# Splitting a pair of weight chunks in fewer, longer operations, from three long ring buffers

## The chip, the core and the metric

The kernel runs on one core of a Trainium2 chip. The time is the device time of one execution in microseconds; the profile is of one execution on the same core.

## The reference

A two-layer decoder trunk in float32, 256 tokens, width 2048, 16 heads of 128, hidden width 8192. Layer 0 mixes by a short gated convolution, layer 1 by stick-breaking attention over keys and values that are made from layer 0's output; each is followed by a squared-ReLU MLP, and every sub-layer stands between two RMS norms.

```python
def reference(x, a_w_in, a_conv_w, a_w_out, kv_norm_g, w_kv, b_w_q, b_w_o, ...):
    h = x
    for i in range(2):
        u = rmsnorm(h, mix_pre_g[i])
        if i == 0: # proj = u @ w_in; y = gate_b * conv3(gate_c * xin); y @ w_out
            m = short_conv_mixer(u, a_w_in[0], a_conv_w[0], a_w_out[0])
        else:      # q = u @ w_q; stick-breaking weights of q, k; (a @ v) @ w_o
            m = stick_breaking_mixer(u, b_w_q[0], k_sh, v_sh, b_w_o[0])
        h = h + rmsnorm(m, mix_post_g[i])
        u = rmsnorm(h, mlp_pre_g[i])
        h = h + rmsnorm(jnp.square(jax.nn.relu(u @ w_up[i])) @ w_down[i], mlp_post_g[i])
        if i == 0:
            k_sh, v_sh = split(rmsnorm(h, kv_norm_g) @ w_kv)
    return h
```

## The kernel before

All products with weights are made in a float32 of two parts. A number is split into a high part (rounded to the format that TensorE multiplies at full rate) and a low part (the number less its high part); a product is high x high, high x low and low x high, three matmuls into one PSUM bank. The activations are split once. The weights, some 400 MB, pass through the chip once and are split on the way.

**The stream.** All weights lie in HBM as chunks of 128 x 1024 float32 (512 KB) in the order of their use. `load_one` issues the load of the next chunk on the SP queue into one of 5 raw tiles (`RAW`). `high_parts` makes a chunk's high part on ScalarE (L173) and `low_part` the low part on VectorE (L184, or L186 where a gain is multiplied in), into one of 7 tiles each (`RING`). `chunk(i)`, called where TensorE's matmuls are written, first writes down the splits up to chunk i + 4 (`AHEAD`; i + 2 in the first chunks). A split waits for its ring slot, which comes free when the last matmul on it is done. A raw tile comes free when its readers are done, and its next load follows.

**Pairs in seven products.** Where two consecutive chunks are a pair, they hold the four 128 x 512 quarters b11, b12 (first chunk), b21, b22 (second) of a block that is multiplied with four blocks of activations by the Strassen-Winograd scheme: 7 products in place of 8, 21 matmuls. The activations' sums are made by `four_sums`, the weights' differences by `split_seven`: t1 = b12 - b11, t3 = b22 - b12, t2 = b22 - t1, t4 = b21 - t2, each a 128 x 512 operation on VectorE (L210) into a tile `sums` that exists once. Then come four splits in four ring slots: a (b11 alone, half a slot), b (the whole second chunk, b21 and b22), t (t1, t2), u (t3, t4): four ScalarE operations (L218), four VectorE operations (L184). `seven_products` lists the products in the order b11, b21, b22, t1, t2, t3, t4.

**Where pairs stand.** In the convolution's projection 16 pairs alternate with 16 of the 26 tiles of output features (a tile takes two chunks; matmuls L748, pairs L857 to L859); a tile's bank is emptied by a ScalarE copy of one half (L755) and a VectorE addition (L757), and the same bank 6 serves every tile between pairs. In each MLP the down-projection's pairs (L1120 to L1122) alternate with tiles of the up-projection (32 matmuls, L1013 high and L1020 low); a tile's bank is emptied by L1026 (ScalarE) and L966 (VectorE) and bank 2 serves every tile. An MLP has 51 pairs in seven products, a few in eight. Partial results of a pair's products are added in SBUF by DMAs from the POOL queue (L1030).

**Order of the work.** TensorE's order is as written. The other engines are ordered by a scheduler at build time, by priority (order of writing, with some blocks raised), and each then runs its queue in order. At the transitions between sub-layers VectorE and ScalarE run in written order too: `Norms.begin` splits up to a limit, `allow(n)` raises it, and `at(delay, ...)` places steps by a planned clock that `spent` advances; with `apart` set, low parts are written separately by `low_parts`.

Of the kernel before, what the change touches and what calls it, by code (L numbers as in the profile page):

```python
# [12 lines left out]
ALU = mybir.AluOpType  # L13
# [82 lines left out]
def trunk(ctx, tc, x, xT, vecs, rows, ws, out):  # L96
# [45 lines left out]

    raw, parts, early = {}, {}, {}
    last_load = [None]
    count = {"loaded": 0, "split": 0, "limit": 1 << 30, "apart": False}
    lows = []
    sevens = {}

    def load_one():
        i = count["loaded"]  # L150
        if i >= len(stream):
            return
        w, c = stream[i]
        t = wpool.tile([P, CW], F32, tag="raw", name=f"raw{i}")
        n = HALF if i < FIRST else CW
        for a in range(0, CW, n):
            last_load[0] = nc.sync.dma_start(t[:, a : a + n], w.ap[c, :, a : a + n])
        raw[i] = t
        count["loaded"] += 1

    def pieces_of(i):
        w, c = stream[i]
        gains = w.gains(c) if w.gains else [None] * (4 if i < FIRST else 1)
        n = CW // len(gains)
        return [(slice(j * n, (j + 1) * n), gain) for j, gain in enumerate(gains)]

    def high_parts(i):
        while count["loaded"] <= i:
            load_one()
        hi = wsplit.tile([P, CW], F32R, tag="hi", name=f"whi{i}")  # L170
        lo = wsplit.tile([P, CW], F32R, tag="lo", name=f"wlo{i}")
        for j, (at, gain) in enumerate(pieces_of(i)):
            rounded = nc.scalar.activation(  # L173
                hi[:, at], raw[i][:, at], AF.Copy, scale=1.0 if gain is None else gain
            )
            if j < 2:
                early[i] = rounded
            if not count["apart"]:
                low_part(hi, lo, raw[i], at, gain)
        parts[i] = hi, lo  # L180

    def low_part(hi, lo, t, at, gain):
        if gain is None:
            nc.vector.tensor_tensor(lo[:, at], t[:, at], hi[:, at].bitcast(F32), op=ALU.subtract)  # L184
        else:
            nc.vector.scalar_tensor_tensor(  # L186
                lo[:, at], t[:, at], gain, hi[:, at].bitcast(F32), op0=ALU.mult, op1=ALU.subtract
            )

    def low_parts(until=None):  # L190

        while lows and (until is None or lows[0] <= until):
            i = lows.pop(0)
            for at, gain in pieces_of(i):
                low_part(*parts[i], raw[i], at, gain)
            raw.pop(i)
            load_one()
            if until is None:
                break

    def split_seven(i):

        while count["loaded"] <= i + 1:
            load_one()
        a, b = raw.pop(i), raw.pop(i + 1)
        sums = sevens[i].tile([P, 4, HALF], F32, tag="gpre", name="sums", bufs=1)
        t1, t2, t3, t4 = (sums[:, j, :] for j in range(4))
        b11, b12, b21, b22 = a[:, :HALF], a[:, HALF:], b[:, :HALF], b[:, HALF:]
        for t, x, y in ((t1, b12, b11), (t3, b22, b12), (t2, b22, t1), (t4, b21, t2)):
            nc.vector.tensor_tensor(t, x, y, op=ALU.subtract)  # L210
        factors = []
        for name, src in (("a", b11), ("b", b[:]), ("t", sums[:, 0:2, :]), ("u", sums[:, 2:4, :])):
            n = 1 if name == "a" else 2
            src = src if n == 1 or name == "b" else src.rearrange("p a b -> p (a b)")
            hi = wsplit.tile([P, CW], F32R, tag="hi", name=f"whi{i}{name}")
            lo = wsplit.tile([P, CW], F32R, tag="lo", name=f"wlo{i}{name}")
            at = slice(0, n * HALF)
            nc.scalar.activation(hi[:, at], src, AF.Copy)  # L218
            low_part(hi, lo, src, at, None)
            factors += [(hi[:, j * HALF : (j + 1) * HALF], lo[:, j * HALF : (j + 1) * HALF]) for j in range(n)]  # L220
        parts[i] = factors
        count["split"] += 2
        load_one()
        load_one()

    def split_one():
        i = count["split"]
        if i in sevens:
            split_seven(i)
            return  # L230
        high_parts(i)
        count["split"] += 1
        if count["apart"]:
            lows.append(i)
        else:
            raw.pop(i)
# [29 lines left out]
    def four_sums(to, a11, a21, a12, a22):  # L266
        s1, s2, s3, s4 = to
        for t, v, w, op in (
            (s1, a21, a22, ALU.add), (s2, s1, a11, ALU.subtract), (s3, a11, a21, ALU.subtract), (s4, a12, s2, ALU.subtract),
        ):  # L270
            nc.vector.tensor_tensor(t, v, w, op=op)

    def seven_products(x, sums, factors):

        b11, b21, b22, t1, t2, t3, t4 = factors
# [26 lines left out]
    def allow(n):  # L302

        count["limit"] += n
        while count["split"] <= count["limit"]:
            split_one()

    class Group:
# [29 lines left out]
        def both(self, i):  # L338

            for b in range(NB):  # L340
                self.unit(b, i)

        def last_units(self, b, edge):

            for c in range(2):
                for i in range(self.n - edge, self.n):
                    self.half(b, c, i)
                    if i == self.n - 1:
                        self.evict(b, c, self.ps.pop((b, c)))
                    spent(UNIT / 2)  # L350

    def run(groups, enter=False, leave=None):
# [3 lines left out]
        for b in range(NB):  # L356
            for gr, i in units[:first]:
                gr.unit(b, i)
        for gr, i in units[first:last]:
            if i == 0 and gr.start is not None:  # L360
                gr.start()
            gr.both(i)
# [343 lines left out]
    def convolution(tmp):  # L706
# [106 lines left out]
        for k in range(KD):  # L813
# [8 lines left out]
            elif k % 2 and k + 2 < KD:  # L822
                enter(k + 1)
                enter(k + 2)
            mm([(ps, k, n) for ps, n in zip(pss, IN_N[:LEAD])], lambda k, n: at_lead[k, n])
            if k % 2 and LATER <= k + 2 < KD:
                squares((k + 2 - LATER) // 2, k + 2)
# [23 lines left out]
        def pair(i):  # L851
# [4 lines left out]
            for key, (xh, xl), (hi, lo) in seven_products(x, sums[q], chunk(IN_AT["pair", i])):  # L856
                nc.tensor.matmul(group[key][:], xh, hi, start=q == 0, stop=False)  # L857
                nc.tensor.matmul(group[key][:], xh, lo, start=False, stop=False)
# [28 lines left out]
        for kind, i in IN_UNITS:  # L887
# [8 lines left out]
            behind = i < 4 or i >= KD + 4  # L896
            mm([(ps, k, n) for k in range(KD)], lambda k, n: at * CH + k, (1, 0) if behind and i % 2 == 0 else (0, 1))
            if not scale:
                statistics()
# [39 lines left out]
    def mlp(pool, i, before, after):  # L939
# [93 lines left out]
        def lead_up(to):  # L1033
# [7 lines left out]
            for k, n in alone:  # L1041
                low(first, place[k, n], k, n)
            for k in range(ALONE, KD):
                for n in lead:
                    high(first, place[k, n], k, n, n + 2)
                for n in lead:
                    low(first, place[k, n], k, n)
                    if k == KD - 1:
                        finish(to, n)
# [3 lines left out]
        def whole_up(to, n, first, number):  # L1053
            for k in range(KD):
                high(first, k, k, n, number)
            for k in range(KD):
                low(first, k, k, n)
            finish(to, n)

# [40 lines left out]
        class Down:  # L1100
# [40 lines left out]
            def seven(self, at, first, xs, n):  # L1141
                x = [[xs.x(n + j, b) for b in range(NB)] for j in range(2)]
                for key, a, w in seven_products(x, xs.sums[n], chunk(first)):
                    own = {1: "more", 5: "fifth", 6: "more", 7: "more"}.get(key, "sum")
                    self.products(key, own, at, [(a, w)])
                spent(3.5 * UNIT)

            def eight(self, at, first, xs, n):
# [12 lines left out]
                else:  # L1161
                    products((0, 1), "sum", lambda t: [xs.sums[n][:, t, j, :] for j in range(2)], 1)
                    products(5, "fifth", lambda t: xs.x(n + t, 1), 1)
                spent(4 * UNIT)

# [246 lines left out]


def banded(w, cols=CW):

# [61 lines left out]
```

## Time and profile before

| | us |
|---|---|
| median of three runs | 2111.22 |
| lowest, highest | 2110.32, 2113.54 |
| the profiled execution | 2110.45 |
| its span, first to last instruction | 2108.7 |

The profiled execution's own time includes about 1.75 us outside the span. The profile gives for each engine its busy time and number of instructions, for each group of instructions the source line, the tiles, the count, the summed and the mean time, and the idle time of the engine ahead of them with what ended it. Matmuls overlap their neighbours, and so do VectorE's and ScalarE's instructions at their ends: the time that one takes of its engine is read from start to start.

### The profile page before, as it was taken

To read this page: it belongs to the slowest core of one execution; us is meant where nothing else is said; L and a number is where in the kernel's file an instruction comes from. 1 tells how busy PE (TensorE), PEld (TensorE's weight loads), DVE (VectorE), ACT (ScalarE), POOL (GpSimd) and SP (SyncE) were. 2 spreads that over 40 slices of the span, in tenths; PEclk is the share of its full clock that TensorE was granted. 3 is DMA by queue.
4 is the path that set the end of the run, shared out by engine and by line. 5 is a ranking of instruction groups with operands and counts; after the bars stand their busy time and mean duration, and the time that the engine had idled before them with its cause. 6 is when DMAs were issued, how large, how long until landed. Compare 5 with 4: busy or idle time off the path is not lost.

```text
span 2108.7 us, 29835 instructions
## 1 busy us (share of the span) xinstructions
PE 2090.4 (99%) x10608; PEld 1782.2 (85%) x10608; DVE 1835.2 (87%) x2807; ACT 1435.2 (68%) x2210; POOL 113.7 (5%) x137
## 2 busy tenths in 40 slices
PE   9999999999999999999999999999999999999998
PEld 8888888888888888888888888889888888888886
DVE  9999965999899999999866777558989999999997
ACT  8656544776776776767567888547767767677674
POOL 0000000010110110101000000000101001011010
PEclk9999999999999999999999999999999999999999
DMA  8467574586777867868575555655778688687683
GB/s 290 155 205 250 191 259 142 190 244 213 232 230 223 265 194 236 250 205 268 173 222 165 160 160 166 218 175 170 199 237 238 213 239 242 210 255 215 220 267 137
DMA packets 132342, 449.23 MB, mean 213 GB/s; under 512 B 14816, under 2 KB 15072, under 8 KB 131168
## 3 DMA queue, kind: packets, MB, share of 16 engines
q1 hardware_dynamic: 113184, 406.55, 58.7%
q0 software_dynamic: 18720, 40.38, 9.9%
q8 instruction: 83, 1.36, 0.3%
q14 instruction: 67, 0.55, 0.1%
q10 hardware_dynamic: 288, 0.39, 0.1%
HBM read 413.19 MB, written 2.10 MB: 197 GB/s over the span
## 4 chain that ended last, share of the span: by engine, by line
PE 91%; DVE 6%; DMA 2%; issue 1%; ACT 1%; DVEq 0%; ACTq 0%
PE up L1013 20%; PE up L1020 11%; PE acc L326 8%; PE acc L328 8%; PE acc L327 8%; PE acc L748 5%; PE more L1121 4%; PE more L1120 4%; PE more L1122 4%; PE acc L1120 4%; PE acc L1121 4%; PE acc L1122 4%; PE lead L748 2%; DVE wlo L184 1%; DMA raw<-w_mlp 1%; PE up L1015 1%
## 5 line engine op out<-in xcount | busy, mean ns | idle before, releaser
L184 DVE TENSOR_TENSOR wlo<-raw,whi 128x1024 fp32r<-128x1024 f32 (+1 forms) x442 | 528.1, 1206 | 87.0 <-ACT whi L173 86.6
L173 ACT ACTIVATE whi<-raw 128x1024 fp32r<-128x1024 f32 (+1 forms) x442 | 453.0, 1043 | 171.1 <-PE acc L328 82.5
L1013 PE MATMUL up<-u,whi 128*128 128x512 f32 x1952 | 465.6, 390 | 3.5 <-DVE s L966 3.5
L1013 PEld LDWEIGHTS up<-u,whi 128*128 128x128 f32 x1952 | 364.6, 188 | 79.9 <-DVE s L966 5.4
L1020 PEld LDWEIGHTS up<-u,wlo 128*128 128x128 f32 x2048 | 263.6, 191 | 10.3
L1020 PE MATMUL up<-u,wlo 128*128 128x256 f32 x2048 | 268.0, 283 | 0.0
L1030 POOL DMA_DIRECT2D mg<-more x108 | 101.7, 1051 | 1280.5 <-ACT s L968 648.3
L186 DVE SCALAR_TENSOR_TENSOR wlo<-raw,gv,whi 128x512 fp32r<-128x512 f32 (+1 forms) x160 | 131.9, 854 | 41.5 <-ACT whi L173 40.8
L210 DVE TENSOR_TENSOR sums<-raw,sums 128x512 f32<-128x512 f32 x236 | 162.1, 687 | 1.3
L173 ACT ACTIVATE whi<-raw,gv 128x512 fp32r<-128x512 f32 (+1 forms) x160 | 121.6, 800 | 48.5 <-PE acc L328 41.8
L326 PE MATMUL acc<-whi,u 128*128 128x512 f32 x384 | 153.1, 399 | 0.1
L328 PE MATMUL acc<-whi,u 128*128 128x512 f32 x384 | 150.0, 391 | 0.0
L327 PE MATMUL acc<-wlo,u 128*128 128x512 f32 x384 | 149.8, 390 | 0.0
L1026 ACT ACTIVATE half<-up 128x256 f32<-128x256 f32 x128 | 48.5, 381 | 89.1 <-PE up L1020 85.5
L748 PE MATMUL acc<-u,whi 128*128 128x512 f32 x416 | 98.9, 391 | 2.7 <-DVE sum L757 2.7
L210 DVE TENSOR_TENSOR sums<-raw,raw 128x512 f32<-128x512 f32 x118 | 81.0, 687 | 23.2 <-DMA raw<-w_mlp 23.0
L967 ACT ACTIVATE s<-s 128x256 f32<-128x256 f32 x128 | 52.4, 413 | 66.3 <-DVE s L966 65.9
L748 PEld LDWEIGHTS acc<-u,whi 128*128 128x128 f32 x416 | 77.4, 188 | 20.5 <-DVE sum L757 3.7
L210 DVE TENSOR_TENSOR sums<-raw 128x512 f32<-128x512 f32 x118 | 81.0, 686 | 11.9 <-DMA raw<-w_mlp 11.7
L328 PEld LDWEIGHTS acc<-whi,u 128*128 128x128 f32 x384 | 72.1, 188 | 15.6
L326 PEld LDWEIGHTS acc<-whi,u 128*128 128x128 f32 x384 | 72.2, 188 | 13.8 <-ACT tk L1309 0.6
L327 PEld LDWEIGHTS acc<-wlo,u 128*128 128x128 f32 x384 | 72.3, 188 | 13.4
(5995 smaller groups left out, 4513.4 us busy)
## 6 DMA issues: line engine op xcount, KB each, us to landing
raw<-w_mlp SPq DMA_DIRECT2D x512, 512.0 KB, 4.6
raw<-w_in SPq DMA_DIRECT2D x94, 512.0 KB, 4.4
mg<-more POOLq DMA_DIRECT2D x108, 256.0 KB, 8.3
raw<-w_out SPq DMA_DIRECT2D x32, 512.0 KB, 4.5
raw<-w_v SPq DMA_DIRECT2D x32, 512.0 KB, 4.3
raw<-w_k SPq DMA_DIRECT2D x32, 512.0 KB, 4.4
raw<-w_q SPq DMA_DIRECT2D x32, 512.0 KB, 4.2
raw<-w_wo SPq DMA_DIRECT2D x32, 512.0 KB, 3.7
```

What stands on the lines that cost most here:

```text
L173: rounded = nc.scalar.activation(hi[:, at], raw[i][:, at], AF.Copy, scale=1.0 if gain is None else gain)
L184: nc.vector.tensor_tensor(lo[:, at], t[:, at], hi[:, at].bitcast(F32), op=ALU.subtract)
L210: nc.vector.tensor_tensor(t, x, y, op=ALU.subtract)
L326: nc.tensor.matmul(ps[:], xh, hi[:, a], start=i == 0 and k == 0, stop=False)
L327: nc.tensor.matmul(ps[:], xh, lo[:, a], start=False, stop=False)
L328: nc.tensor.matmul(ps[:], xl, hi[:, a], start=False, stop=i == self.n - 1 and k == self.ks - 1)
L748: nc.tensor.matmul(ps[:, :cols], w, xs[:, :cols], start=k == 0 and part == parts[0], stop=k == KD - 1 and part == parts[1], skip_group_che ...
L1013: nc.tensor.matmul(ps, weight(0, first, m), x, start=k == 0, stop=False)
L1020: nc.tensor.matmul(pss[n][:, :T], weight(1, first, m), x, start=False, stop=k == KD - 1)
L1120: nc.tensor.matmul(self.ps[key][:], xh, hi, start=first, stop=False)
L1121: nc.tensor.matmul(self.ps[key][:], xh, lo, start=False, stop=False)
L1122: nc.tensor.matmul(self.ps[key][:], xl, hi, start=False, stop=last)
```

## The change

The 5 raw tiles become one tile `raws` of 5 x 1024 columns, the 7 high and 7 low tiles one tile `his` and one tile `los` of 14 halves (512 columns) each. A chunk's raw place is its number modulo 5. Ring places are given out by halves in order of use (`ring_halves`), and a count of free halves is kept: `used(n)`, written after the matmuls that use them last, gives n halves back and calls `fill`, which writes down the next splits as long as the target is not reached and enough halves are free (2 for a chunk, 3 and then 4 for a pair). `chunk` and `allow` only raise the target and call `fill`.

A pair is split in two steps. `sums_of_weights` makes the differences, t1 and t3 in one operation of two rows where the pair's raw halves lie in a row, with b12 read by broadcast (t3 has the other sign, and so has its sum of activations in `four_sums`); then it splits b11, b21, b22 together, which is possible as the host now stores a pair's first chunk with its halves exchanged (b12, b11), so that the three lie in a row. When four halves are free, the second step splits the four differences: two high parts of 1024 columns, one low part of 2048. `runs` cuts an operation where the raw places or the ring places don't continue. The products' order is b11, b21, b22, t1, t3, t2, t4.

```diff
-    wpool = ctx.enter_context(tc.tile_pool(name="w", bufs=RAW))
-    wsplit = ctx.enter_context(tc.tile_pool(name="ws", bufs=RING))
+    wpool = ctx.enter_context(tc.tile_pool(name="w", bufs=1))
+    wsplit = ctx.enter_context(tc.tile_pool(name="ws", bufs=1))
...
+    raws = wpool.tile([P, RAW * CW], F32, name="raws")
+    his = wsplit.tile([P, 2 * RING * HALF], F32R, name="whi")
+    los = wsplit.tile([P, 2 * RING * HALF], F32R, name="wlo")
+
+    def raw_halves(i):
+        return [(raws, i % RAW * 2 + j) for j in range(2)]
+
+    def ring_halves(n):
+        assert count["free"] >= n
+        first = count["half"]
+        count["half"] += n
+        count["free"] -= n
+        return [(first + j) % (2 * RING) for j in range(n)]
...
+    def runs(src, dst):
+
+        k = 0
+        while k < len(src):
+            n = 1
+            while k + n < len(src) and all(
+                (src[k + n][0] is src[k][0], src[k + n][1] == src[k][1] + n, dst[k + n] == dst[k] + n)
+            ):
+                n += 1
+            yield src[k][0][:, src[k][1] * HALF : (src[k][1] + n) * HALF], slice(dst[k] * HALF, (dst[k] + n) * HALF)
+            k += n
...
-    def split_seven(i):
+    def sums_of_weights(i):
 
         while count["loaded"] <= i + 1:
             load_one()
-        a, b = raw.pop(i), raw.pop(i + 1)
-        sums = sevens[i].tile([P, 4, HALF], F32, tag="gpre", name="sums", bufs=1)
-        t1, t2, t3, t4 = (sums[:, j, :] for j in range(4))
-        b11, b12, b21, b22 = a[:, :HALF], a[:, HALF:], b[:, :HALF], b[:, HALF:]
-        for t, x, y in ((t1, b12, b11), (t3, b22, b12), (t2, b22, t1), (t4, b21, t2)):
-            nc.vector.tensor_tensor(t, x, y, op=ALU.subtract)
-        factors = []
-        for name, src in (("a", b11), ("b", b[:]), ("t", sums[:, 0:2, :]), ("u", sums[:, 2:4, :])):
...
-            nc.scalar.activation(hi[:, at], src, AF.Copy)
-            low_part(hi, lo, src, at, None)
...
+        (_, b12), (_, b11), (_, b21), (_, b22) = raw_halves(i) + raw_halves(i + 1)
+        sums = sevens[i].tile([P, 4 * HALF], F32, tag="gpre", name="sums", bufs=1)
...
+        if b22 == b11 + 2:
+            nc.vector.tensor_tensor(
+                total(0, 2).rearrange("p (a n) -> p a n", a=2),
+                of(b12).unsqueeze(1).to_broadcast([P, 2, HALF]),
+                of(b11, 3).rearrange("p (a n) -> p a n", n=HALF)[:, 0:3:2, :], op=ALU.subtract,
+            )
+        else:
+            nc.vector.tensor_tensor(total(0), of(b12), of(b11), op=ALU.subtract)
+            nc.vector.tensor_tensor(total(1), of(b12), of(b22), op=ALU.subtract)
+        nc.vector.tensor_tensor(total(2), of(b22), total(0), op=ALU.subtract)
+        nc.vector.tensor_tensor(total(3), of(b21), total(2), op=ALU.subtract)
+        begun.append(sums)
+        parts[i] = split_halves(raws, (b11, b21, b22), 1)
         load_one()
         load_one()
 
+    def split_halves(src, at, n_high):
+
+        halves = ring_halves(len(at))
+        src = [(src, j) for j in at]
+        n = len(at) // n_high
+        for a in range(0, len(at), n):
+            for x, to in runs(src[a : a + n], halves[a : a + n]):
+                nc.scalar.activation(his[:, to], x, AF.Copy)
+        for x, to in runs(src, halves):
+            low_part(x, to, None)
+        return [[ring[:, j * HALF : (j + 1) * HALF] for ring in (his, los)] for j in halves]
+
+    def needed():
+        return (4 if begun else 3) if count["split"] in sevens else 2
+
     def split_one():
         i = count["split"]
+        if begun:
+            parts[i] += split_halves(begun.pop(), range(4), 2)
+            count["split"] += 2
+            return
...
+    def fill():
+        while count["split"] <= min(count["target"], len(stream) - 1) and count["free"] >= needed():
+            split_one()
+
+    def used(halves=2):
+
+        count["free"] += halves
+        fill()
+
     def chunk(i, low=True):
-        while count["split"] <= min(i + (AHEAD if i >= CALM else 2), len(stream) - 1, max(i, count["limit"])):
-            split_one()
+        count["target"] = max(count["target"], min(i + (AHEAD if i >= CALM else 2), max(i, count["limit"])))
+        fill()
...
-            (s1, a21, a22, ALU.add), (s2, s1, a11, ALU.subtract), (s3, a11, a21, ALU.subtract), (s4, a12, s2, ALU.subtract),
+            (s1, a21, a22, ALU.add), (s2, s1, a11, ALU.subtract), (s3, a21, a11, ALU.subtract), (s4, a12, s2, ALU.subtract),
...
-            (1, x[0][0], b11), ((0, 0), x[1][0], b21), ((0, 1), s4, b22), (5, s1, t1), (6, s2, t2), (7, s3, t3),
+            (1, x[0][0], b11), ((0, 0), x[1][0], b21), ((0, 1), s4, b22), (5, s1, t1), (7, s3, t3), (6, s2, t2),
...
                 for key, a, w in seven_products(x, xs.sums[n], chunk(first)):
                     own = {1: "more", 5: "fifth", 6: "more", 7: "more"}.get(key, "sum")
                     self.products(key, own, at, [(a, w)])
+                    used(1)
...
+def second_first(pair):
+    return np.stack([np.concatenate([pair[0][:, HALF:], pair[0][:, :HALF]], axis=1), pair[1]])
```

The other matmul loops call `used` in the same way after a chunk's last matmul: the lead and the tiles of the convolution, `Group.both` and `last_units`, `lead_up`, `whole_up`, and pairs in eight products (4 halves at once).

More of the change, by code (lines that the diff above doesn't have):

```diff
@@ L169, in high_parts @@
             load_one()
[L170 to L175, printed above, removed]
+        halves = ring_halves(2)
+        parts[i] = Part(his, halves), Part(los, halves)
+        for j, (x, to, gain) in enumerate(pieces_of(i)):
+            rounded = nc.scalar.activation(his[:, to], x, AF.Copy, scale=1.0 if gain is None else gain)
             if j < 2:
@@ L193, in low_parts @@
             i = lows.pop(0)
-            for at, gain in pieces_of(i):
-                low_part(*parts[i], raw[i], at, gain)
-            raw.pop(i)
+            for x, to, gain in pieces_of(i):
+                low_part(x, to, gain)
             load_one()
@@ L304, in allow @@
         count["limit"] += n
-        while count["split"] <= count["limit"]:
-            split_one()
+        count["target"] = max(count["target"], count["limit"])
+        fill()
     class Group:
@@ L825, in convolution @@
             mm([(ps, k, n) for ps, n in zip(pss, IN_N[:LEAD])], lambda k, n: at_lead[k, n])
+            for _ in range(k * LEAD // CH, (k + 1) * LEAD // CH):
+                used()
             if k % 2 and LATER <= k + 2 < KD:
@@ L1445 @@
     arrays["w_in"] = np.concatenate([tiled(w_in, IN_LEAD)] + [
-        bands[2 * i : 2 * i + 2] if kind == "pair" else tiled(w_in, [(k, IN_TILES[i]) for k in range(KD)])
+        second_first(bands[2 * i : 2 * i + 2]) if kind == "pair" else tiled(w_in, [(k, IN_TILES[i]) for k in range(KD)])
         for kind, i in IN_UNITS
@@ L1460 @@
         downs = [banded(w) for w in np.split(a["mlp_w_down"][i], STEPS, axis=0)]
+        for e, down in enumerate(downs):
+            for h in range(2):
+                for m in SEVEN[e][h]:
+                    pair = slice(8 * band_of(e, h) + 2 * m, 8 * band_of(e, h) + 2 * m + 2)
+                    down[pair] = second_first(down[pair])
         arrays[f"w_mlp{i}0"] = ups[0]
```

71 lines of the change are left out of this document (48 added, 23 removed).

## Prediction

> **What bounds the kernel now.** I read the page first: the span, the engines' busy time, the slices, the chain.
>
> ```profile
> span 2108.7 us, 29835 instructions
> PE 2090.4 (99%) x10608; PEld 1782.2 (85%) x10608; DVE 1835.2 (87%) x2807; ACT 1435.2 (68%) x2210; POOL 113.7 (5%) x137
> DVE  9999965999899999999866777558989999999997
> PE 91%; DVE 6%; DMA 2%; issue 1%; ACT 1%; DVEq 0%; ACTq 0%
> ```
>
> TensorE is busy 99% of the span and the chain of waits is 91% TensorE. The change leaves every matmul in place, so the most that it can win is the time in which TensorE stands still. VectorE is busy 87% on average, but its slices are full in the convolution's second half and in both MLPs. So the second view was the sums by stage, the third TensorE's waits (matmul rows, then weight-load rows), and beside them the wait of the differences for loads.
>
> ```profile
> core 0: us, PE busy (x) PEld busy (x) DVE busy (x) ACT busy (x) POOL busy (x), PEclk, DMA share, GB/s
> 50.00:200.00 150.00, 147.28 (x757) 124.97 (x756) 149.92 (x234) 91.60 (x122) 1.23 (x2) 1.00 0.61 200
> 560.00:990.00 430.00, 430.00 (x2204) 368.82 (x2203) 407.62 (x591) 305.16 (x462) 40.12 (x46) 1.00 0.77 233
> ...
> PE acc L748 <- DVE sum L757: 4.7, 5, 1.9
> PE up L1013 <- DVE s L966: 3.5, 4, 1.8
> ...
> PEld acc L748 <- DVE sum L757: 5.8, 5, 2.2
> PEld up L1013 <- DVE s L966: 5.4, 5, 2.2
> ...
> DVE sums L210 <- DMA raw<-w_mlp: 34.7, 27, 2.7
> ```
>
> From 50 to 200 us VectorE has no idle time (149.92 of 150.00) and TensorE loses 150.00 - 147.28 = 2.7 us; in the middle of the first MLP TensorE loses nothing (430.00 of 430.00) and VectorE has 5% free (407.62). All that TensorE loses to VectorE is 4.7 + 3.5 = 8.2 us by the matmul rows, 5.8 + 5.4 = 11.2 us by the weight-load rows. Each is the same kind: a PSUM bank cannot be reused because VectorE adds its two halves (L757, L966) late. None of these rows is a wait for a weight part. The gain therefore ends at 8 to 11 us, however much VectorE work goes.
>
> **What the change removes.** The split of one pair of weight chunks in seven products is 4 differences and 4 low parts on VectorE, 4 high parts on ScalarE.
>
> ```profile
> L184 DVE TENSOR_TENSOR wlo<-raw,whi 128x1024 fp32r<-128x1024 f32 x434 | 525.0, 1221 | 86.7 <-ACT whi L173 86.4 <-issue 0.2
> L173 ACT ACTIVATE whi<-raw 128x1024 fp32r<-128x1024 f32 x434 | 450.1, 1054 | 170.8 <-PE acc L328 82.5 <-PE up L1013 30.4 <-DMA raw<-w_mlp 15.8
> L210 DVE TENSOR_TENSOR sums<-raw,sums 128x512 f32<-128x512 f32 x236 | 162.1, 687 | 1.3
> L210 DVE TENSOR_TENSOR sums<-raw,raw 128x512 f32<-128x512 f32 x118 | 81.0, 687 | 23.2 <-DMA raw<-w_mlp 23.0
> L210 DVE TENSOR_TENSOR sums<-raw 128x512 f32<-128x512 f32 x118 | 81.0, 686 | 11.9 <-DMA raw<-w_mlp 11.7
> ```
>
> So there are 118 pairs; by the loops 16 of them are in the convolution and 51 in each MLP. Merging two 512-column operations into one of 1024 takes 2 x 687 - 1221 = 153 ns off the busy sum. But neighbouring operations overlap in the profile, so the true saving is read from their starts:
>
> ```profile
> 705.97 0.69 DVE L210 TENSOR_TENSOR sums<-raw,raw 128x512 f32<-128x512 f32 x1
> 706.57 0.69 DVE L210 TENSOR_TENSOR sums<-raw,sums 128x512 f32<-128x512 f32 x1
> 707.17 0.69 DVE L184 TENSOR_TENSOR wlo262a<-raw,whi262a 128x512 fp32r<-128x512 f32 x1
> ...
> 708.59 1.22 DVE L184 TENSOR_TENSOR wlo262b<-raw,whi262b 128x1024 fp32r<-128x1024 f32 x1
> 709.72 1.22 DVE L184 TENSOR_TENSOR wlo262t<-sums,whi262t 128x1024 fp32r<-128x1024 f32 x1
> 710.85 1.22 DVE L184 TENSOR_TENSOR wlo262u<-sums,whi262u 128x1024 fp32r<-128x1024 f32 x1
> ```
>
> 512 columns cost 0.60 us from start to start, 1024 cost 1.13: a merge saves 2 x 0.60 - 1.13 = 0.07 us of VectorE.
>
> How many merges happen follows from the rings. The first two differences merge unless the pair lies across the end of the five raw chunks: 4 in 5, 0.80. The low parts of b11, b21, b22 become one operation if the raw halves are in a row (4 in 5) and three ring halves are too (12 of 14 starts): 0.69. The four differences' low parts become one in 11 of 14 starts: 0.79. Against that, a pair uses 7 of 14 halves, so the places turn odd and a plain chunk is cut by the ring's end in 1 of 14 cases, two chunks for each pair: -0.14. Sum 2.14 merges for a pair, 252 VectorE instructions in all: 252 x 0.153 = 39 us less in the busy sum (1835 to about 1797), but 252 x 0.07 = 18 us of VectorE's time. ScalarE saves 0.69 - 0.14 - 0.14 = 0.4 instructions for a pair, about 48; it is 68% busy and off the path, so zero, with its idle 32% as cover.
>
> The new two-row difference reads one operand by broadcast and the other with a hole between its rows; the trace has no such read. Its bounds are 1.13 us (a plain 1024) and 1.20 us (the two it replaces), more only if the form is slow; I take 1.13, since L210 and L184 show the same time for the same 512 columns whatever their operands. If it cost 1.13 more, the convolution's 16 pairs would lose 18 us of VectorE there.
>
> **What that is worth.** In the MLPs nothing: VectorE has 5% free and TensorE waits in four places only (3.5 us), each behind a queue of low parts at a moment when loads come late. In the convolution VectorE is full, so its saving counts: 16 x 2.14 x 0.07 = 2.4 us, bounded by the 4.7 us of waits there. One of them stands at the end of the lead tiles, before any pair, in the waits of the first 45 us:
>
> ```profile
> PE acc L748 <- DVE sum L757: 1.9, 1, 1.9
> ```
>
> That stays; 2.8 is left. I take -2.0 here and -1.0 of the 3.5 in the MLPs.
>
> **What the change adds.** First, a part of a weight comes later: the low part of b11 now ends with those of b21 and b22, and the low part of t1 with that of all four differences. In the steady MLP this is covered:
>
> ```profile
> 714.72 0.40 PE L1120 MATMUL more<-whi262a,hid 128*128 128x512 f32 x1
> ...
> 715.64 0.39 PE L1121 MATMUL acc<-wlo262b,hid 128*128 128x512 f32 x1
> ```
>
> The low part of b21 (262b) ends at 708.59 + 1.22 = 709.8 and is read at 715.64, 5.8 us later. That is the cover; without it each product would wait about 1 us. In the convolution the cover is nearly gone:
>
> ```profile
> 98.09 1.22 DVE L184 TENSOR_TENSOR wlo32t<-sums,whi32t 128x1024 fp32r<-128x1024 f32 x1
> 99.05 0.36 ACT L755 ACTIVATE half<-acc 128x256 f32<-128x256 f32 x1
> 99.22 1.22 DVE L184 TENSOR_TENSOR wlo32u<-sums,whi32u 128x1024 fp32r<-128x1024 f32 x1
> 99.57 0.40 PE L858 MATMUL more<-wlo32t,xsums 128*128 128x512 f32 x1
> 100.36 2.36 DVE L184 TENSOR_TENSOR wlo<-raw,whi 128x1024 fp32r<-128x1024 f32 x2
> 102.63 0.42 DVE L757 TENSOR_TENSOR sum<-acc,half 128x256 f32<-128x256 f32 x1
> 103.10 1.21 PE L748 MATMUL acc<-u,whi 128*128 128x512 f32 x4 [0.86 <-DVE sum L757]
> ```
>
> The low part of t1, t2 ends at 99.31 and is read at 99.57. As one operation with t3, t4 it would end near 99.22 + 1.22 - 0.07 = 100.37: TensorE would wait 0.8 us. But VectorE's queue does not get longer by that: the eviction behind it still starts at about 102.6, so the 0.86 us wait at 103.10 shrinks by the same 0.8. Where VectorE is the late one, the wait only changes its place. I charge +1.0 us in all for pairs where no eviction wait follows.
>
> Second, a split is now issued only when the planner knows 3, 4 or 2 halves of the ring to be free, and what is moved with it are its loads on SP (two for a pair). A pair with its two tile chunks takes 7 + 4 = 11 of 14 halves, where it took 4 + 2 = 6 of 7 slots: the ring has room for 14/11 = 1.27 periods instead of 1.17. Following the counts: three halves come free when the tile ends, four more after four products, so the first step runs at the start of the pair before and the second at its end, half a period or more ahead of use. Cost zero; cover is the 5.8 us above.
>
> Third, the raw halves of a pair's first chunk, released so far by the low part of b11 (262a, ends 707.17 + 0.69 = 707.86), wait for the common one (709.8 or a little earlier): that load starts up to 2 us later. SP issues nothing else, so nothing is queued behind but the next loads, which follow it anyway. Covered by the same 5.8 us, which exceeds 2 us.
>
> **The sum.** The profiled execution took 2110.45 us: 2108.7 of span and 1.75 outside it, 0.77 under the median of the three runs, 2111.22. Moves: -2.0 - 1.0 + 1.0 = -2.0. On the median that is 2109.2; I say 2109. A measurement of this kernel can tell about 0.2%, 4.2 us, from no change, so this is "same".
>
> **Rivals.**
> *The stalls all go* (25% for faster by more than 4.2 us). For it: all TensorE waits on VectorE are evictions behind a full queue. Against: the 1.9 us at the lead stays, and one needs two thirds of the other 6.3. Time 2111.2 - 8.2 = 2103, by the weight-load rows 2100.
>
> *The longer operations make the waits* (20%, slower). Place: the convolution's 16 pairs and the first pair of each MLP, 18 places where VectorE is just in time. Price: 0.8 us each as at 99.57, 14 us together: 2125. It decides where a low part's lead over its reader is under about 1 us and no eviction wait follows to take it back. Against it: VectorE's work there falls. The Trainium skill (Perfetto Trace Analysis, "Optimizing Scalar/DVE Operations") says for this that breaking up instructions may let work finish sooner where Scalar or Vector are not saturated but cause bubbles elsewhere, the opposite of this change; by that rule the MLPs (VectorE 95% full) would lose, and the trace's 5.8 us of lead speaks against it there, while at 50 to 200 us VectorE is saturated and the rule's condition is not met.
>
> *Loads become late* (13%, slower). Differences already wait 34.7 us for loads, 27 times. The merged one needs both chunks at once, one of them issued 2 us later, and VectorE is held in order meanwhile, with evictions behind it. Priced at 2 us in the 4 MLP places that already stall: +8, 2119. It decides when the delay eats the lead of 5.8 us; 2 does not, alone.
>
> *The change doesn't merge as counted*: ring cuts everywhere would leave 2111, inside "same".
>
> **How the numbers follow.** 42% same, 25% faster, 33% slower. The range takes in the faster rival but for its outer end and the slower one nearly whole: 2102 to 2124; the likeliest case alone has 2107 to 2113 (all of the 2.8 and half of the 3.5 gone; or nothing gone and 1 to 2 us of new waits).
>
> **What would show it.** Right: VectorE's busy sum near 1797, about 250 fewer VectorE instructions, TensorE still x10608, the L757 waits down to 2 to 3 us with 1.9 at the lead. The longer operations show as TensorE waiting for low parts (wlo) in the convolution; late loads as more than 34.7 us of differences waiting for loads and more L966 waits. Wrong altogether: a new VectorE or ScalarE wait for TensorE of tens of us, which would mean that the ring's bookkeeping holds the splits back, or TensorE time lost in the steady MLP.

## The result, and the profile after

The changed kernel takes 2140.68 us (median of 4 runs, 2138.1 to 2144.64) against 2110.77 us for the kernel before in the same comparison: 1.0143 times as long, 95% interval 1.013 to 1.0155. It is 30 us slower; 2109 was forecast, and the range ended at 2124.

The page of the profile after, its first lines, VectorE's slices and the chain by engine:

```profile
span 2142.9 us, 29457 instructions
PE 2104.3 (98%) x10608; PEld 1784.0 (83%) x10608; DVE 1824.4 (85%) x2576; ACT 1425.4 (67%) x2184; POOL 113.8 (5%) x137
DVE  8998965989898998898865777658989999998997
PE 71%; DVE 16%; DMA 6%; issue 3%; ACT 3%; DVEq 0%; SPq 0%; ACTq 0%
```

VectorE does do less: 231 fewer instructions and 11 us less busy time. But it is no longer full (8s where 9s stood), and the chain leaves TensorE for 29% of the span: it goes over VectorE 16% and over DMA 6%, where it was 6% and 2%. An engine that has less to do and is at the same time waited for more may well be waiting itself; the rows further down show that it is. TensorE's waits, matmul rows and then weight-load rows (total, times, longest):

```profile
PE more L1210 <- DVE wlo L227: 13.4, 8, 3.1
PE up L1096 <- DVE s L1049: 6.4, 9, 1.8
...
PEld more L1210 <- DVE wlo L227: 17.1, 9, 3.5
PEld up L1096 <- DVE s L1049: 13.9, 19, 2.2
PEld more L939 <- DVE wlo L227: 6.0, 7, 2.8
PEld acc L827 <- DVE sum L836: 3.7, 4, 2.1
```

The four weight-load rows give 40.7 us, where two rows gave 11.2 before: 29.5 us of the 34.2 us by which the span grew (2142.9 - 2108.7). L1210 and L939 are waits for low parts of weights, a kind that the kernel before hardly had; L1049 is the old L966, the up-projection's bank that is emptied late. The clock adds to it: the mean granted clock is 0.996 where it was 0.999, and 0.3% of 2142.9 us is 6 us. The two overlap in part, as their sum, 35.5 us, is a little more than what the span grew by.

What the other engines wait for, loads above all:

```profile
ACT whi L279 <- DMA raws<-w_mlp: 89.7, 53, 4.7
ACT whi L219 <- DMA raws<-w_mlp: 38.3, 34, 4.6
DVE sums L257 <- DMA raws<-w_mlp: 20.9, 13, 3.8
```

ScalarE stands 128 us waiting for loads in the MLPs (89.7 + 38.3). In the kernel before, the same two kinds of operation waited 53 us: 15.8 for plain chunks (L173) and 37.2 for pairs (L218). VectorE's waits for loads fell meanwhile from 34.7 us to 22. The loads themselves are not slower: their median from issue to landing in the MLPs is 4.5 us, 4.6 before, and 35 of the 512 take 8 us or more, 41 before. They go out a little later, on average 4.5 matmuls or about 1 us (counted in both traces by the matmuls begun when a load is issued). One place in the timeline shows what a late one does:

```profile
732.40 1.49 ACT L279 ACTIVATE whi<-raws 128x1536 fp32r<-128x1536 f32 x1 [3.22 <-DMA raws<-w_mlp]
733.79 0.36 ACT L1109 ACTIVATE half<-up 128x256 f32<-128x256 f32 x1
734.19 0.42 DVE L1049 TENSOR_TENSOR s<-up,half 128x256 f32<-128x256 f32 x1 [1.55 <-ACT half L1109]
734.66 1.65 PE L1096 MATMUL up<-u,whi 128*128 128x512 f32 x6 [0.32 <-DVE s L1049]
```

The high part of b11, b21, b22 is one operation now and reads both chunks of the pair. It stands at the head of ScalarE's queue for 3.22 us until the second chunk has landed (issued at 723.47, landed 8.8 us later). Behind it in the queue is the copy that empties TensorE's bank (L1109), whose tile was finished long before; behind that the addition on VectorE, and behind that TensorE.

A second place, where VectorE makes TensorE wait:

```profile
483.87 0.68 DVE L266 TENSOR_TENSOR sums<-raws,sums 128x512 f32<-128x512 f32 x1
484.47 2.35 DVE L227 TENSOR_TENSOR wlo<-raws,whi 128x1024 fp32r<-128x1024 f32 x2
484.59 1.06 ACT L279 ACTIVATE whi<-sums 128x1024 fp32r<-128x1024 f32 x1 [0.33 <-DVE sums L266]
486.75 2.28 DVE L227 TENSOR_TENSOR wlo<-sums,whi 128x2048 fp32r<-128x2048 f32 x1
489.08 0.50 PE L1210 MATMUL more<-wlo,hid 128*128 128x512 f32 x1 [3.10 <-DVE wlo L227]
```

The low parts of all four differences are one operation, so it needs the high part of the last difference t4, which is made at 483.87 and rounded at 484.59. Meanwhile VectorE takes up two other low parts, and the product with t1 gets its low part 3.1 us late.

### The profile page after: what moved, and what is told of

Its sections match the earlier page's. It is cut to its first block, busy times and chain, and to the rows that moved or that the text cites. A ratio compares the mean times of both kernels' runs of the same rounds, so it can differ in the third digit from the quotient of the medians.

```text
span 2142.9 us, 29457 instructions
## 1 busy us (share of the span) xinstructions
PE 2104.3 (98%) x10608; PEld 1784.0 (83%) x10608; DVE 1824.4 (85%) x2576; ACT 1425.4 (67%) x2184; POOL 113.8 (5%) x137
## 4 chain that ended last, share of the span: by engine, by line
PE 71%; DVE 16%; DMA 6%; issue 3%; ACT 3%; DVEq 0%; SPq 0%; ACTq 0%
PE up L1096 14%; DVE wlo L227 9%; PE up L1103 8%; PE acc L400 7%; PE acc L402 7%; PE acc L401 7%; DMA raws<-w_mlp 5%; PE more L1210 3%; PE more L1211 3%; PE more L1209 3%; PE acc L1209 3%; PE acc L1210 3%; PE acc L1211 3%; PE acc L827 2%; DMA raws<-w_in 1%
## 5 line engine op out<-in xcount | busy, mean ns | idle before, releaser
L227 DVE TENSOR_TENSOR wlo<-raws,whi 128x1024 fp32r<-128x1024 f32 (+3 forms) x633 | 739.0, 1184 | 86.9 <-ACT whi L219 84.4
L219 ACT ACTIVATE whi<-raws 128x1024 fp32r<-128x1024 f32 (+2 forms) x475 | 457.7, 983 | 177.6 <-PE acc L402 80.6
L227 DVE TENSOR_TENSOR wlo<-sums,whi 128x2048 fp32r<-128x2048 f32 (+3 forms) x141 | 272.9, 1939 | 48.5 <-ACT whi L279 47.2
L279 ACT ACTIVATE whi<-sums 128x1024 fp32r<-128x1024 f32 (+1 forms) x251 | 250.4, 1002 | 63.2 <-DVE sums L257 27.7
L279 ACT ACTIVATE whi<-raws 128x1536 fp32r<-128x1536 f32 (+2 forms) x158 | 182.2, 1160 | 144.9 <-DMA raws<-w_mlp 89.7
L1113 POOL DMA_DIRECT2D mg<-more x108 | 100.9, 1024 | 1308.7 <-ACT s L1051 431.3
L229 DVE SCALAR_TENSOR_TENSOR wlo<-raws,gv,whi 128x512 fp32r<-128x512 f32 (+1 forms) x164 | 132.9, 838 | 43.8 <-ACT whi L219 43.3
L401 PE MATMUL acc<-wlo,u 128*128 128x512 f32 x384 | 149.7, 390 | 0.0
L219 ACT ACTIVATE whi<-raws,gv 128x512 fp32r<-128x512 f32 (+1 forms) x164 | 124.0, 790 | 35.9 <-PE acc L402 30.6
L257 DVE TENSOR_TENSOR sums<-raws 128x1024 f32<-128x1024 f32 x95 | 115.7, 1218 | 21.1 <-DMA raws<-w_mlp 20.9
L1210 PE MATMUL acc<-wlo,hid 128*128 128x512 f32 x288 | 113.2, 393 | 0.1
L1209 PE MATMUL acc<-whi,hid 128*128 128x512 f32 x288 | 113.3, 393 | 0.0
L1211 PE MATMUL acc<-whi,hid 128*128 128x512 f32 x288 | 112.4, 390 | 0.0
L1210 PE MATMUL more<-wlo,hid 128*128 128x512 f32 x238 | 94.4, 397 | 13.4 <-DVE wlo L227 13.4
```

The source lines that it names most:

```text
L219: rounded = nc.scalar.activation(his[:, to], x, AF.Copy, scale=1.0 if gain is None else gain)
L227: nc.vector.tensor_tensor(los[:, to], x, his[:, to].bitcast(F32), op=ALU.subtract)
L279: nc.scalar.activation(his[:, to], x, AF.Copy)
L401: nc.tensor.matmul(ps[:], xh, lo[:, a], start=False, stop=False)
L1209: nc.tensor.matmul(self.ps[key][:], xh, hi, start=first, stop=False)
L1210: nc.tensor.matmul(self.ps[key][:], xh, lo, start=False, stop=False)
```

## The experiments

**All operations short again, rings kept.**

```diff
-        if b22 == b11 + 2:
+        if False:                                     # four differences of 512
...
-        parts[i] = split_halves(raws, (b11, b21, b22), 1)
+        parts[i] = split_halves(raws, (b11, b21, b22), (1, 2), (1, 2))   # sizes of high, of low parts
...
-            parts[i] += split_halves(begun.pop(), range(4), 2)
+            parts[i] += split_halves(begun.pop(), range(4), (2, 2), (2, 2))
```

`split_halves` takes the sizes of its high and of its low parts here; that part of the diff is left out, and the remarks behind # are added.

> The changed kernel with every long operation of a pair's split cut as it was before: four differences of 512 columns, b11 apart from b21 and b22 in high and low parts, the low parts of t1, t2 apart from those of t3, t4. The rings, the counting of free halves and the exchanged halves stay. Theory A (the long operations make the waits, above all the low parts of the four differences in one operation): back to 2109 to 2116 us, TensorE's waits for low parts (13.4 + 3.2 us in the matmul rows) under 2 us. Theory B (splits are written down later and loads are issued later because of the ring's counts): stays at 2130 us or more, loads still 5 to 15 matmuls later in the MLPs.

Measured: 2114.06 us, ratio 1.0009 (0.9999 to 1.0019) to the kernel before. No TensorE wait for low parts in the MLPs is left:

```profile
PE acc L834 <- DVE sum L843: 4.9, 5, 1.7
PE up L1103 <- DVE s L1056: 3.1, 6, 1.1
```

These are the two rows of the kernel before (4.7 and 3.5). So the rings, the counting of free halves and the exchanged halves together cost nothing that can be told from the noise, and all of the loss but some 3 us is in the long operations. Theory B has fallen. ScalarE still waits 81 us for loads in the MLPs here (57.6 + 23.3): such waits cost time only where something that TensorE needs soon stands behind them.

**One long operation taken back.** From the changed kernel: the last low parts as (2, 2) again, and the first high part as (1, 2) again.

> The changed kernel with one edit: the low parts of t1, t2 and of t3, t4 are two operations of 1024 columns again. Theory A in its narrow form (the 2048-column low part waits for the high part of t3, t4 and ends 1 to 3 us later than the product with t1 needs it): 13 to 20 us faster than the changed kernel, 2120 to 2127 us, and TensorE's wait for low parts under 4 us. Theory B: within 4 us of 2140. If the high part over three halves, which waits for the second chunk's load, is the cause (theory C): within 6 us of 2140, since that stays.

> The changed kernel with one edit: ScalarE makes the high part of b11 apart from that of b21, b22 (the low parts stay in one operation). Theory C (ScalarE's queue stands at the three-half high part until the pair's second chunk has landed, 89.7 us of waiting for loads at that line, and the eviction copies behind it come late): 8 to 15 us faster, 2125 to 2132 us, waits for L1049's successor down from 6.4 to about 3.5 us. Theory A narrow: within 4 us of 2140, since VectorE still waits for both. Theory B: within 4 us of 2140.

Measured: cutting the last low parts made it slower still, 2165.18 us (1.0246, 1.0223 to 1.0269); cutting the high part gave 2132.8 us (1.0107, 1.0083 to 1.0131). The first missed all three expectations. The second ended just outside theory C's range, 7.9 us under the change with intervals that touch, and not by the way that C named: the waits for evictions rose from 6.4 to 8.6 us in place of falling to 3.5, and those for low parts fell from 16.6 to 9.6 us:

```profile
PE up L1103 <- DVE s L1056: 8.6, 10, 1.9
PE more L1217 <- DVE wlo L227: 5.0, 5, 2.1
```

So the high part alone is not the cause. The waits of the first, the last low parts cut, show what took over there:

```profile
PE up L1103 <- DVE s L1056: 40.0, 30, 5.4
...
DVE sums L257 <- DMA raws<-w_mlp: 77.5, 44, 4.3
```

and one instance in its timeline:

```profile
725.60 1.49 ACT L285 ACTIVATE whi<-raws 128x1536 fp32r<-128x1536 f32 x1 [3.38 <-PE acc L1218]
725.62 1.22 DVE L257 TENSOR_TENSOR sums<-raws 128x1024 f32<-128x1024 f32 x1 [2.75 <-DMA raws<-w_mlp]
727.00 0.36 ACT L1116 ACTIVATE half<-up 128x256 f32<-128x256 f32 x1
728.50 0.42 DVE L1056 TENSOR_TENSOR s<-up,half 128x256 f32<-128x256 f32 x1
728.97 2.37 PE L1103 MATMUL up<-u,whi 128*128 128x512 f32 x9
```

Low parts of t1 are in time now, but the two-row difference stands at the head of VectorE's queue for 2.75 us, the three-half high part at the head of ScalarE's for 3.38, and both leave in the same 0.02 us: the pair's second chunk has landed. (The profile puts ScalarE's wait down to a matmul that ended then too; which of the two was last cannot be told from this row.) The eviction comes behind both. From here the theory was D: operations that join both chunks of a pair hold an in-order queue until the later load.

**Earlier loads.** 6 raw chunks and 13 ring halves, long operations kept:

```diff
-RAW = 5
+RAW = 6
...
-    his = wsplit.tile([P, 2 * RING * HALF], F32R, name="whi")
+    his = wsplit.tile([P, 13 * HALF], F32R, name="whi")
...
```

> The changed kernel with 6 raw chunks in place of 5 and 13 ring halves in place of 14 (the memory has no room for both). If late loads are what matters (B or C): ScalarE's waits for loads (89.7 + 38.3 us in the MLPs) fall by half or more and the time to 2120 to 2130 us. If the long low part alone (A): 2135 to 2145 us. If the ring's room matters more than the loads: slower than 2145 us.

Measured: 2126.63 us (1.007, 1.0055 to 1.0086). ScalarE's waits for loads in the MLPs went from 128 to 17 us and the wait for the eviction (L1049) left TensorE's list. What was left is mostly waits for low parts, nearly half of them at a new place, the start of the projections of keys and values (L401):

```profile
PE acc L401 <- DVE wlo L229: 7.3, 2, 5.8
PE more L1210 <- DVE wlo L227: 5.8, 2, 3.0
```

**Each kind of long operation alone.** All short but one kind: the last low part of 2048 columns; the two-row difference; the three-half high and low parts of b11, b21, b22.

> The changed kernel with the whole first step cut as before (differences of 512, b11 apart from b21, b22 in high and low parts); of the long operations only the low part of the four differences, 2048 columns, is left. Theory D (an operation that needs both chunks of a pair stands at the head of its engine's queue until the second chunk has landed, and the eviction and low parts behind it come late): 2111 to 2118 us, since nothing here needs both chunks more than before. Theory A narrow (the 2048-column low part is late for the product with t1): 2125 us or more with TensorE waits for low parts over 8 us.

> The changed kernel with all cut as before except the two-row difference (t1 and t3 in one operation, which needs both chunks). Theory D: 2125 to 2165 us, with VectorE's wait for loads at the two-row difference near the 77.5 us that it had where only the last low part was cut, and TensorE waiting for L966's successor by 20 us or more. If D is wrong and the three-half operations do it: 2112 to 2118 us.

> The changed kernel with the differences and the last low parts cut as before; the high and low parts of b11, b21, b22 stay one operation each. Theory D: 2118 to 2135 us, through ScalarE, whose three-half high part needs both chunks ahead of the eviction's copy (57.6 us of waiting for loads with short operations, some 85 here). If only the two-row difference matters: 2112 to 2117 us.

| kernel | us | ratio to before, 95% interval |
|---|---|---|
| all short | 2114.06 | 1.0009 (0.9999 to 1.0019) |
| only the 2048-column low part | 2116.73 | 1.0024 (1.0014 to 1.0035) |
| only the three-half parts | 2125.43 | 1.0067 (1.0049 to 1.0086) |
| only the two-row difference | 2134.95 | 1.0112 (1.0097 to 1.0127) |
| all long but the last low part | 2165.18 | 1.0246 (1.0223 to 1.0269) |
| the change | 2140.68 | 1.0143 (1.013 to 1.0155) |

The two-row difference, one instruction fewer for a pair, costs 21 us by itself (2134.95 - 2114.06), the three-half parts 11 us. In both the eviction is what TensorE waits for, first the difference's and then the parts' waits:

```profile
PE up L1103 <- DVE s L1056: 15.8, 11, 3.9
DVE sums L257 <- DMA raws<-w_mlp: 51.0, 29, 5.2
...
PE up L1103 <- DVE s L1056: 8.6, 8, 2.9
ACT whi L285 <- DMA raws<-w_mlp: 81.3, 47, 5.0
```

The 15.8 us fell short of the 20 that I had written for the difference, and VectorE's 51.0 us of the 77.5. Of the 15.8, 12.2 us are four late evictions of 2.2 to 3.9 us, near 560, 982, 1635 and 2061 us, and behind the last two the granted clock fell to half (0.50 from 1636 to 1640 us and from 2062 to 2066 us). The price of a merge is paid in a few places, not a little in each of the 95.

A rival is that the scheduler, given other operations, puts the evictions at other places of the queues. The traces speak against it for the difference: beside the kernel with all short, the eviction's copy on ScalarE stands behind the same number of halves of weight splits in 124 of the 128 tiles of the up-projections, and the addition on VectorE in 101, in 19 of the others behind one half more.

The long last low part, which waits for no load that its halves did not wait for before, costs 2.7 us by the medians, and the two intervals overlap a little. The costs don't add up: 21 + 11 gives 32, the kernel with both has 51, and all three together 27. For the last the order does differ: with the long last low part, alone (77 of 128 tiles) or with the two others (87), the addition stands 1 to 4 halves further forward in VectorE's queue than in the kernel with all short. That this is why the third long operation makes the other two cheaper is likely, but no run isolates it.

**The loads made quick.** The partial products are added in SBUF by DMAs from the POOL queue, in bursts, and during a burst loads land late (those that the changed kernel issues from 719 to 726 us, 7.9 to 11.5 us after their issue). The kernels here leave these additions out:

```diff
-                    nc.gpsimd.dma_start(a, more, accum_op=ALU.add)
+                    pass
```

> The changed kernel without the 108 DMAs that add partial products in SBUF (that part of the computation is left out). They are what makes a load land 8 to 11 us after its issue instead of 4 to 5. Theory D (an operation that needs both chunks stands in its queue until the second has landed): waits for loads fall to a third, TensorE's waits fall to those of the convolution, and the time to 2112 to 2122 us. If the long operations are slow in themselves or badly placed whatever the loads do: 2130 us or more.

> The kernel before without the same 108 DMAs (that part is left out): the reference for the two other kernels without them. TensorE's 3.5 us of waits for L966 in the MLPs go: 2105 to 2109 us in every theory.

> The slowest variant (long operations, but the last low parts cut; 2165 us) without the same 108 DMAs (that part is left out). Theory D: its 40 us of TensorE waits behind evictions fall under 10 us and the time to 2110 to 2122 us, near the changed kernel without them. If the order that the scheduler gives this variant is bad by itself: 2140 us or more.

Measured: the change 2119.41 us, the kernel before 2107.63, the slowest variant 2119.66. All three times fell where D had them. No load of the MLPs takes 8 us any more, and the order of VectorE's and ScalarE's queues is the same as with the additions, so it is the loads that changed. The variant gains 45.5 us and the change 21 by the same edit, the kernel before 3, and the two with long operations meet: the 24 us between them come only with late loads. What D said of the waits held less well: in the change ScalarE's and VectorE's waits for loads fell to two fifths (from 150 to 62.5 us), not a third, and TensorE kept a wait in the MLPs. The variant's waits beside the 40.0 and 77.5 above:

```profile
DVE sums L257 <- DMA raws<-w_mlp: 33.8, 26, 3.0
PE up L1103 <- DVE s L1056: 8.3, 7, 2.5
```

A part that does not come from the bursts remains, 11.8 us (2119.41 - 2107.63). In the change without the additions TensorE waits thus:

```profile
PE more L1210 <- DVE wlo L227: 3.4, 3, 1.6
PE more L939 <- DVE wlo L227: 3.3, 4, 2.4
```

The first row is the product with t1 in the MLPs, the second in the convolution; they make 6.7 of the 11.8 us. The 6 raw chunks give the same size by another way: 2126.63 long against 2116.89 short, 9.7 us, with 8.8 us of waits for low parts in the same two places.

**Short operations and six raw chunks.** Short operations, with 6 raw chunks and 13 halves, and then the same with one low part written earlier at the place of the 7.3 us:

```diff
             allow(1)
+            low_parts()
             self.due.append(what)
```

> All operations short as before, 6 raw chunks and 13 ring halves. If the waits for loads are what is left of TensorE's stalls behind evictions, they go: 2104 to 2109 us, faster than the kernel before. If 13 halves are too few at the transitions (7.3 us of waits at the start of the keys' and values' projections with 6 raw chunks): 2110 to 2118 us.

> All operations short, 6 raw chunks, 13 ring halves, and one more low part written down early where the keys' and values' projections begin. With 6 raw chunks and short operations TensorE's waits were 7.3 us at that place, 3.5 us in the convolution and none in the MLPs. If the low part there was late only by its place in VectorE's order: 2104 to 2109 us. If the ring of 13 is too small there: no change from 2117.

Measured: 2116.89 us (1.0025, 1.0015 to 1.0035), with the 7.3 us at L408 and no wait in the MLPs; and with the low part in place 2107.85 us, 0.9987 of the kernel before (0.9978 to 0.9996). That is 33 us faster than the change, and about 3 us faster than the kernel before by an interval that only just leaves out no difference. The sixth chunk alone did not gain: the low part that came late by its place in VectorE's order had to move too. Two of TensorE's waits for VectorE in it, the largest and what is left at the place of the 7.3 us:

```profile
PE acc L835 <- DVE sum L844: 3.5, 4, 0.9
PE acc L408 <- DVE wlo L229: 0.3, 1, 0.3
```

So what the rings were good for is not the merging: counted by halves, they work with 13 where tiles took 14, and the half that this frees in each of the two, 2 x 512 columns, is the room of a sixth raw chunk.

## Why the prediction was wrong

*The bound.* Right: the matmuls stayed (x10608), and TensorE's stalls set the time. That a gain ends at 8 us was not put to the test: the best version reached 3.

*The merges.* The count was nearly right: 95 two-row differences (0.80 x 118 = 94 were worked out), 84 three-half low parts (81), 95 of 2048 columns (93), and 231 fewer instructions for 252; the rest is cuts of plain chunks at the ring's end, which happen outside the pairs too. The time of one was right for the difference, 1.218 us on average like a plain 1024. VectorE's busy sum is where a step was wrong: 153 ns for a merge gave 1797, measured 1824.4. The busy sum already counts an overlap once, so the 0.07 us from the starts comes nearer: 231 x 0.07 = 16 for 11 measured.

*"Cost zero" for the counting.* Right, as the kernel with all operations short shows.

*The failed step* is what I wrote under what the change adds: that 5.8 us of lead cover both the later parts and the later loads. That lead was measured between a low part and its reader in TensorE's program. The wait of a merged operation has another reader: whatever stands behind it in its own queue, and that is the eviction of the up-projection's bank. Its lead is one pair's products, 21 matmuls from the end of the tile to the next one, 4.6 us in the traces, of which the copy and the addition themselves take 0.8; and loads alone are waited for by up to 4.7 us in the change. Counted in the traces, of the 98 such evictions 5 end more than 4.5 us after the tile in the kernel before, 10 with all short, 13 with the three-half parts, 19 with the difference, 21 in the change, 37 in the slowest variant and none in the change with 6 raw chunks. The rival *loads become late* named this wait ("VectorE is held in order meanwhile, with evictions behind it") and got 13%; it was also priced wrongly, at 2 us in 4 places, 8 us. The price was read from places that already stalled, not from the 27 waits of differences for loads that the page showed, each of which a merged operation could turn into a late eviction. Measured: 21 us for the difference alone, 11 us for the three-half parts. And the sum has no term for the three-half high part's wait on ScalarE, whose 32% of idle time I called cover; idle time is no cover for an engine whose next instruction cannot start. The sign that I named for wrong altogether came, time of TensorE lost in the steady MLP, but what I said it would mean, that the ring's bookkeeping holds the splits back, did not.

*The longer operations make the waits* was right in kind for about a third of the loss (9.7 to 11.8 us by two ways, of which 8.8 and 6.7 are such waits): a fused low part ends with its last member. Alone, though, the 2048-column low part cost only 2.7 us, so how much of the third is its own stays open. The 14 us were sized from 18 places; TensorE waited in 12 by the rows for L1210 and L939 (8 + 4), with up to 3.1 us each. Eight of them stand in the MLPs, none at the first pair, where the rival had put them; that the sizes are near is luck. The rule that was quoted beside it, from the Trainium skill (Perfetto Trace Analysis, "Optimizing Scalar/DVE Operations"), to break instructions up where an engine is not saturated but causes bubbles elsewhere, is what the runs bear out: with all cut as before, 2114 instead of 2141. I set it aside because of the 5.8 us.

*The evictions in the convolution.* Right in kind: the waits for the addition of a tile's halves fell from 4.7 to 3.3 us by the matmul rows, while waits for low parts there (3.2) took their place.

What stays open: why the change with its last low part cut is 24 us slower than the change. The experiment without additions says that it takes late loads. The traces show another order too: in 78 of 128 tiles the addition stands behind 1 to 5 more halves of weight splits in VectorE's queue than in the change (on ScalarE the copy's place is the same in 125). That the two together make the 24 us is likely, but no run isolates the order.

## What to carry to other kernels

Before merging two operations on an engine that runs its queue in order, ask when each input arrives and what stands next in that queue: the merged operation starts with the later input and ends with the last member, and everything behind it waits too. A saving in instructions was worth nothing here, on an engine that is not the bound: VectorE did 11 us less and the kernel took 30 us more. And where loads come in bursts of lateness, one more buffer for raw data can be worth more: with short operations and one low part moved it made 2107.85 of 2114.06 us.

## What was unexpected in the hardware

Stalls of TensorE of 2 to 3 us can cost more than themselves. After the wait of 3.1 us near 486 us the granted clock fell for a few microseconds (windows; the last three columns are the clock, the DMA share and GB/s):

```profile
484.00:488.00 4.00, 1.98 (x9) 1.30 (x7) 4.00 (x4) 1.89 (x3) 0.00 (x0) 1.00 0.82 242
488.00:492.00 4.00, 2.92 (x8) 2.36 (x9) 4.00 (x8) 2.97 (x6) 0.00 (x0) 0.72 0.75 283
492.00:496.00 4.00, 4.00 (x16) 3.22 (x16) 3.30 (x3) 3.07 (x3) 0.00 (x0) 0.86 0.54 153
```

A mean of 0.72 and 0.86 over two windows of 4 us is a loss of 0.28 x 4 + 0.14 x 4 = 1.7 us of full-speed time, on top of the 3.1. The same is seen after a wait of 2.1 us near 1981 us (0.85 and 0.73 in the two windows behind it). Not every stall does it: with the difference alone, those of 2.2 and 2.6 us near 560 and 982 us were followed by windows at 1.00. The slowest variant has a mean clock of 0.995, the kernel before 0.999.
